# An attention stage with its score products on 64 rows, its query unstacked and its values between zeros

## The chip, the cores and the metric

The kernel runs on one core of a Trainium2 chip. Its time is that of one launch on the device, in microseconds (us); the time shown is the median of several runs. A profile is one execution that the hardware profiler took. It names the engines PE (TensorE; PEld is its weight loads), DVE (VectorE), ACT (ScalarE), POOL (GpSimd) and SP (SyncE, which here only starts transfers).

## What is computed

An encoder trunk of two layers on 256 tokens of width 1024: each layer is a SwiGLU, a mixer, and a SwiGLU again, each followed by a layer norm. The mixer of the first layer is an mLSTM, that of the second is attention in a window, and only the attention is changed here. It has 16 query heads of size 64 and 4 key heads; four query heads share a key head. Each query sees keys up to 128 tokens away, with a penalty that grows with the distance, and each head has a sink in the denominator. Cut to that:

```python
D_MODEL, SEQ, HEAD_DIM, N_Q_HEADS, N_KV_HEADS, WINDOW = 1024, 256, 64, 16, 4, 128

def window_attention(x, w_in, sink, w_out):
    p = x @ w_in                                   # q, k, v
    ...
    s = jnp.einsum('bnqkgd,bnskd->bnkgqs', q, kw).astype(jnp.float32) * (HEAD_DIM ** -0.5)
    ...
    s = s - slopes[:, :, None, None] * dist
    s = jnp.where(valid[None, :, None, None], s, MASK_VALUE)
    m = jnp.maximum(jnp.max(s, axis=-1, keepdims=True), sink_l)
    pe = jnp.exp(s - m)
    attn = pe / (jnp.sum(pe, axis=-1, keepdims=True) + jnp.exp(sink_l - m))
    o = jnp.einsum('bnkgqs,bnskd->bnqkgd', attn, vw.astype(jnp.float32)).reshape(B, S, nq)
    return o.astype(x.dtype) @ w_out
```

## The kernel before

Six stages follow one another (FFN, mLSTM, FFN, FFN, attention, FFN), and the whole of it is issued from lists. The functions of the stages do not issue instructions, they record them: `Program` collects every operation, and `Program.issue` gives them out in the order of the list `ORDER` (steps between indices of the recorded operations), the same order for all engines. Which buffer of a rotating group an operation uses is written out as well, in `SLOTS`, one digit per use. Both lists were made ahead for the whole kernel. So the order of the program text sets what depends on what, and the lists set how the work of neighbouring steps is interleaved.

All matrix products work on numbers split in two: a value x is kept as hi (x rounded to fp32r) and lo (the rest, x - hi, also fp32r). A product is three matmuls, hi*hi, hi*lo and lo*hi (`mm3`). A split out of a PSUM bank (`split_evac`) is a cast on ScalarE for hi and a subtraction on VectorE for lo. Weights come in as words of 128 x 1024 by the SP queue, wait in rooms for raw weights, and are split by ScalarE and VectorE into a ring of ten (`w_hi`, `w_lo`).

The attention stage (`attn`) works with heads in pairs: pair j holds heads 2j and 2j+1 (called a = 0 and 1), and pairs 2g and 2g+1 share key head g. t counts the two blocks of 128 queries, sb the two blocks of 128 keys.

- `proj`, `k_turn`, `q_turn` and `q_rest` project keys, values and the query, and turn keys and query so that the head's 64 dimensions lie on the partitions. Of a pair's query, head a = 0 then lies on partitions 0 to 63 and head a = 1 on 64 to 127. The keys are put on both halves of the partitions, twice the same.
- `stacked` puts the query of one head into `q2` with hi on partitions 0 to 63 and lo on 64 to 127. One matmul on 128 rows with the doubled keys hi thus gives (hi + lo) * hi; a second one with the keys lo gives the rest. For each head that is one cast on ScalarE and one subtraction on VectorE, each on 64 partitions.
- `scores(j)` takes two PSUM banks, one per query block t, each with both heads side by side. A matmul with the distances (512 columns) opens each bank, four score matmuls of 256 columns follow, and one `reduce_max` on VectorE reads the bank. Small operations make the bias, then four exponentials on ScalarE read the banks.
- `scale(j)` divides by the sum on GpSimd; `turn(j, sb)` transposes on TensorE and splits the result into `pr` (cast now, subtraction with the next `flush`).
- `values(j)` multiplies: the weights are the 128 columns [values hi | values lo] of key head g (tile `va`, `v0` and `v1` in the trace), the moving operand is `pr` hi or lo of both heads, 512 columns, for both key blocks: four matmuls into one bank of 128 x (2, 256). In it, head a = 0 has its hi part on partitions 0 to 63 and its lo part on 64 to 127 of columns 0 to 255, head a = 1 likewise in the other columns. Two copies on ScalarE and two additions on VectorE bring them together in the tile `o`, which is then split into `q2` in the place of the pair's query.
- `out_proj` multiplies that with the output weights, into four PSUM banks that stay taken until the end of the stage. `q_rest` in the first steps and `out_proj` in the later ones are put between as filling.

The loop over `st` runs eleven steps; step st works on the scores of pair st, the scaling of pair st-1, the turning of pair st-2 and the values of pair st-3. PSUM has eight banks in one group (`p`). The stage has six rooms for raw weights, the four common ones and two of its own (`s_raw`).

Of the kernel before, what the change touches and what calls it, by code (L numbers as in the profile page):

```python
# [259 lines left out]
        "792047126847"),  # L260
    "t.0": ("20315553143105122040201230230"),
    "stats": ("110100101010"),
    "mv": ("010011111111"),
    "rs": ("101101010000"),
    "raw.1": ("31030310310213023021012301201320"),
    "wt.1": ("1023"),
# [167 lines left out]
def trunk_kernel(ctx: ExitStack, tc: tile.TileContext, x, ffn_w_in, ffn_w_out, ln_g, ln_b, ml_w_in, ml_gate_b,  # L434
# [207 lines left out]
    def tok(t):  # L642
        return slice(t * 128, (t + 1) * 128)
# [849 lines left out]
```

## Time and profile before

| what | value |
|---|---|
| median of 3 runs | 922.61 us (922.59 to 923.38) |
| the profiled execution | 922.74 us, span of its instructions 921.0 us |
| granted TensorE clock, mean | 0.998 |
| instructions | 12305 |
| VectorE, ScalarE, GpSimd busy | 89%, 63%, 15% of the span |
| read from HBM, written | 206.65 MB, 1.05 MB |
| attention stage | its projections and its last output products lie at about 640 and 738 us |

How to read it: TensorE's instructions overlap one another, so a matmul's own duration is longer than the time from its start to the next one's, and the busy share says little about how densely they follow. A row of the timeline gives start, duration, engine, line, operation, out<-in, the used part of the array, the moving operand's shape and the count; in square brackets stands the idle time in front and what ended it. A row of the groups gives the same kind of names, the count, the busy time with the mean in ns, and the idle time in front. All rows name line 314, the one at which `issue` gives out every operation; so they are told apart by the names of their tiles: out<-in, moving operand first, weights last. `sc` are the exponentials, `pr_hir` and `pr_lor` the turned ones, `q2r` the query and, later, the result, `kk` the keys, `distr` the distances, `p` a PSUM bank.

### The profile page before, as it was taken

What the parts mean: (1) busy time and instruction counts of PE and PEld (TensorE: products, weight loads), DVE (VectorE), ACT (ScalarE), POOL (GpSimd) and SP (SyncE); (2) the same over time, 40 slices, a digit from 0 to 9 for tenths busy, and PEclk for the clock granted to TensorE, in tenths of its full rate; (3) what the DMA queues carried; (4) which work ended last, traced back from release to release, by engine and by line L of the source; (5) the groups of instructions that cost most, each with busy time, mean ns of one, the idle gap of its engine ahead of it and who ended that gap; (6) DMA issues with size and microseconds to landing.
All of it is one profiled execution on the core that took longest, in us unless ns stands there. A gap on an engine that the chain in (4) does not pass through costs nothing.

```text
span 921.0 us, 12305 instructions
## 1 busy us (share of the span) xinstructions
PE 907.0 (98%) x4381; PEld 753.3 (82%) x4381; DVE 818.0 (89%) x964; ACT 580.7 (63%) x818; POOL 142.5 (15%) x198
## 2 busy tenths in 40 slices
PE   8999999999999999999999999999999999999996
PEld 6888888889988888888888888888887788888885
DVE  6999899887789999889999989898899799988986
ACT  6767577445754667566637675675589567666660
POOL 0111121210111112111011112010335311202110
PEclk9999999999999999999999999999999999999999
DMA  9998999567344888899968898976751278998951
GB/s 333 299 242 268 274 283 242 186 203 230 141 168 167 282 249 187 287 262 249 323 224 203 237 289 243 288 184 203 235 202 67 93 228 235 260 305 199 310 131 46
DMA packets 100654, 208.51 MB, mean 226 GB/s; under 512 B 6864, under 2 KB 21216, under 8 KB 100592
## 3 DMA queue, kind: packets, MB, share of 16 engines
q1 hardware_dynamic: 82816, 173.82, 53.7%
q0 software_dynamic: 17632, 33.64, 22.0%
q8 instruction: 34, 0.56, 0.2%
q10 hardware_dynamic: 144, 0.26, 0.1%
q14 instruction: 28, 0.23, 0.1%
HBM read 206.65 MB, written 1.05 MB: 226 GB/s over the span
## 4 chain that ended last, share of the span: by engine, by line
PE 95%; DVE 2%; ACT 1%; DMA 1%; issue 0%; POOL 0%; DVEq 0%; ACTq 0%; SPq 0%; POOLq 0%
PE p L314 95%; DMA w_raw<-in_at_w_out_dram 1%; ACT sc L314 1%; DVE rm L314 1%; DMA x<-in_x_dram 0%; DVE pr_lor L314 0%; DVE x L314 0%; ACT xT_hi L314 0%; ACT pr_hir L314 0%; DVE q2r L314 0%; POOL sc L314 0%; ACT q2r L314 0%; POOL sm L314 0%; DVE nm L314 0%; DVE o L314 0%
## 5 line engine op out<-in xcount | busy, mean ns | idle before, releaser
L314 ACT CAST w_hi<-s_raw 128x1024 fp32r<-128x1024 f32 x243 | 249.6, 1052 | 96.7 <-PE p L314 60.5
L314 DVE TENSOR_TENSOR w_lo<-s_raw,w_hi 128x1024 fp32r<-128x1024 f32 x243 | 289.5, 1219 | 17.3 <-ACT w_hi L314 15.7
L314 ACT CAST w_hi<-w_raw 128x1024 fp32r<-128x1024 f32 (+1 forms) x163 | 168.1, 1042 | 82.2 <-PE p L314 41.4
L314 DVE TENSOR_TENSOR w_lo<-w_raw,w_hi 128x1024 fp32r<-128x1024 f32 (+1 forms) x163 | 194.9, 1210 | 22.1 <-ACT w_hi L314 15.7
L314 PE MATMUL p<-w_hi,xT_hi 128*128 128x512 f32 x512 | 197.8, 396 | 1.3 <-ACT xT_hi L314 0.9
L314 PE MATMUL p<-w_lo,xT_hi 128*128 128x512 f32 x512 | 196.3, 393 | 0.5 <-DVE w_lo L314 0.5
L314 PE MATMUL p<-w_hi,xT_lo 128*128 128x512 f32 x512 | 195.8, 392 | 0.0
L314 PE MATMUL p<-w_hi,h_hir 128*128 128x512 f32 (+1 forms) x323 | 119.6, 392 | 0.0
L314 PE MATMUL p<-w_hi,h_lor 128*128 128x512 f32 (+1 forms) x323 | 118.0, 389 | 0.0
L314 PE MATMUL p<-w_lo,h_hir 128*128 128x512 f32 (+1 forms) x323 | 117.8, 389 | 0.0
L314 PEld LDWEIGHTS p<-w_hi,xT_hi 128*128 128x128 f32 x512 | 96.1, 188 | 21.3 <-ACT xT_hi L314 1.6
L314 PEld LDWEIGHTS p<-w_lo,xT_hi 128*128 128x128 f32 x512 | 96.2, 188 | 19.7 <-DVE w_lo L314 0.9
L314 PEld LDWEIGHTS p<-w_hi,xT_lo 128*128 128x128 f32 x512 | 96.0, 188 | 19.8 <-DVE xT_lo L314 0.9
L314 PE MATMUL p<-w_lo,S_hir 128*128 128x512 f32 x256 | 97.3, 389 | 0.0
L314 PE MATMUL p<-w_hi,S_hir 128*128 128x512 f32 x256 | 96.5, 390 | 0.0
L314 POOL DMA_DIRECT2D s_raw<-in_ffn_w_in_dram x41 | 50.5, 1274 | 291.4 <-DVE w_lo L314 135.2
L314 PE MATMUL p<-w_hi,S_lor 128*128 128x512 f32 x256 | 95.5, 389 | 0.0
L314 PEld LDWEIGHTS p<-w_lo,h_hir 128*128 128x128 f32 x323 | 60.7, 188 | 12.2
L314 PEld LDWEIGHTS p<-w_hi,h_lor 128*128 128x128 f32 x323 | 60.7, 188 | 12.1
L314 PEld LDWEIGHTS p<-w_hi,h_hir 128*128 128x128 f32 x323 | 60.6, 188 | 12.0 <-issue 0.2
L314 POOL DMA_DIRECT2D w_raw<-in_ffn_w_in_dram x23 | 28.9, 1274 | 196.2 <-DVE s_raw L314 74.5
L314 PEld LDWEIGHTS p<-w_hi,S_hir 128*128 128x128 f32 x256 | 48.1, 188 | 10.5 <-ACT t L314 0.6
(195 smaller groups left out, 1220.7 us busy)
## 6 DMA issues: line engine op xcount, KB each, us to landing
s_raw<-in_ffn_w_in_dram SPq DMA_DIRECT2D x103, 512.0 KB, 6.5
s_raw<-in_ffn_w_out_dram SPq DMA_DIRECT2D x57, 512.0 KB, 6.3
w_raw<-in_ffn_w_in_dram SPq DMA_DIRECT2D x56, 512.0 KB, 5.3
s_raw<-in_ffn_w_in_dram POOLq DMA_DIRECT2D x41, 512.0 KB, 7.4
w_raw<-in_ffn_w_out_dram SPq DMA_DIRECT2D x31, 512.0 KB, 6.1
w_raw<-in_ml_w_in_dram SPq DMA_DIRECT2D x24, 512.0 KB, 4.1
w_raw<-in_ffn_w_in_dram POOLq DMA_DIRECT2D x23, 512.0 KB, 7.4
s_raw<-in_ffn_w_in_dram SPq DMA_DIRECT2D x18, 256.0 KB, 5.9
```

The costliest lines, as they stand in the source:

```text
L314: f(*args, **kw)
```

## The change

The query is no longer stacked: `stacked` goes, and one cast and one subtraction on 128 partitions put both heads of a pair into `q2`, hi and lo as two slices. A score product of a head is then three matmuls on 64 rows (hi*hi, hi*lo, lo*hi; the product lo*lo, which the stacking brought along, is not computed any more), on partitions 0 to 63 for a = 0 and on 64 to 127 for a = 1. The two heads are issued in turn. The two banks are now one per head, with both query blocks in it; both are opened by their distances first, and the two `reduce_max` follow when all twelve matmuls are done.

The tile of the values is [hi or lo][576 columns]: nine strips of 64, the values of the four key heads in strips 1, 3, 5 and 7, zeros in the others, filled once by GpSimd. Two neighbouring strips are the weights, [values | zeros] for a = 0 and [zeros | values] for a = 1, so that the two heads come out on partitions 0 to 63 and 64 to 127 of the same 256 columns. Twelve matmuls of 256 columns (three products, two key blocks, two heads) add up in one bank. The copies, the additions and the tile `o` go; the split reads the bank. Since the values take more room, the stage has one raw room of its own instead of two.

`ORDER` (6641 operations before, 6697 after) and all of `SLOTS` are made anew, for the whole kernel.

```diff
@@ the lists
-    "0 10 -9 10 -9 11 -10 11 -5 6 1 -12 13 1 -13 14 1 -14 15 1 -15 16 1 1 1 -18 21 1 -3 92 -88 1 3 102 -109 5 1 "
...
-    "raw.4": ("05121212150432104215"),
+    "raw.4": ("02124141341203402134"),
...
-    "o.4": ("01001001"),
@@ attn
-            va = [tile_([128, 4, 2, 64], FR, f"v{t}") for t in range(2)]
+            va = [tile_([128, 2, 576], FR, f"v{t}") for t in range(2)]
+            for v in va:
+                for e in range(2):
+                    nc.gpsimd.memset(v[:, e].bitcast(F32).rearrange("p (g d) -> p g d", d=64)[:, 0::2], 0.0)
             q2 = tile_([128, 8, 2, S], FR, "q2")
-            rooms.kind(f"raw.{keys[bound[0]]}", raws + pool.new("s_raw", D, 2, F32))
+            rooms.kind(f"raw.{keys[bound[0]]}", raws + pool.new("s_raw", D, 1, F32))
@@ proj
-                    split_evac((va[t][:, :, 0], va[t][:, :, 1]), kv[:, 1])
+                    split_evac(tuple(va[t][:, e].rearrange("p (g d) -> p g d", d=64)[:, 1::2] for e in range(2)), kv[:, 1])
@@ the query
-            def stacked(j, a, m, src, scale=None):
-
-                r = slice(64 * a, 64 * a + 64)
-                split_evac((q2[0:64, j, a, m], q2[64:128, j, a, m]), src[r], scale[r] if scale is not None else None)
-
             def q_turn(t):
                 p = ybank((128, 4, 128))
                 for j in range(4):
                     nc.tensor.transpose(p[:, j], qd[t][:, j], ident)
-                for a in range(2):
-                    stacked(slice(0, 4), a, tok(t), p)
+                split_evac((q2[:, 0:4, 0, tok(t)], q2[:, 0:4, 1, tok(t)]), p)
@@ q_rest
-                        for a in range(2):
-                            stacked(4 + 2 * g + f, a, A, p, qs_col[:, 2 * g + f:2 * g + f + 1])
+                        j = 4 + 2 * g + f
+                        split_evac((q2[:, j, 0], q2[:, j, 1]), p, qs_col[:, j - 4:j - 3])
@@ scores
+                for a in range(2):
+                    nc.tensor.matmul(ps[a], neg_id, dist, start=True, stop=False)
                 for t in range(2):
-                    p = ps[t]
-                    nc.tensor.matmul(p, neg_id, dist[:, t, None, :].to_broadcast([128, 2, S]), start=True, stop=False)
-                    for a in range(2):
-                        for e in range(2):
-                            nc.tensor.matmul(p[:, a], q2[:, j, a, tok(t)], kk[e][:, g], start=False, stop=a == e == 1)
-                    nc.vector.reduce_max(rm[:, t], p, axis=AX.X)
+                    for n_, (qe, ke) in enumerate(((0, 0), (0, 1), (1, 0))):
+                        for a in range(2):
+                            r = slice(64 * a, 64 * a + 64)
+                            nc.tensor.matmul(ps[a][:, t], q2[r, j, qe, tok(t)], kk[ke][r, g], start=False,
+                                             stop=t == 1 and n_ == 2)
+                for a in range(2):
+                    nc.vector.reduce_max(rm[:, :, a], ps[a], axis=AX.X)
...
-                        nc.scalar.activation(s_[:, a], ps[t][:, a], AF.Exp, bias=nm[:, t, a:a + 1],
+                        nc.scalar.activation(s_[:, a], ps[a][:, t], AF.Exp, bias=nm[:, t, a:a + 1],
@@ values
-                p = wbank((128, 2, S))
-                for e in range(2):
-                    for sb in range(2):
-                        v = va[sb][:, j // 2].rearrange("p a d -> p (a d)")
-                        nc.tensor.matmul(p, v, pr[j, sb][e], start=e == sb == 0, stop=e == sb == 1)
-                o = tile_([128, S], F32, "o", bufs=2)
-                top, low = slice(0, 64), slice(64, 128)
-                nc.scalar.copy(o[top], p[top, 0])
-                nc.scalar.copy(o[low], p[low, 1])
-                nc.vector.tensor_add(o[top], p[low, 0], o[top])
-                nc.vector.tensor_add(o[low], p[top, 1], o[low])
-                sums[j] = o
+                p, g = wbank((128, S)), j // 2
+                for n_, (ve, pe, sb) in enumerate((ve, pe, sb) for ve, pe in ((0, 0), (1, 0), (0, 1)) for sb in range(2)):
+                    for a in range(2):
+                        v = va[sb][:, ve, 64 * (2 * g + 1 - a):64 * (2 * g + 3 - a)]
+                        nc.tensor.matmul(p, v, pr[j, sb][pe][:, a], start=n_ == a == 0, stop=n_ == 5 and a == 1)
+                sums[j] = p
```

More of the change, by code (lines that the diff above doesn't have):

```diff
@@ L40 @@
     "0 10 -9 10 -9 11 -10 11 -5 6 1 -12 13 1 -13 14 1 -14 15 1 -15 16 1 1 1 -18 21 1 -3 92 -88 1 3 102 -109 5 1 "
[202 rows of a table removed]
[207 rows of a table added]
 )
 SLOTS = {
-    "raw.0": ("310284657392ab105846a2b0183547691837250843691a72b5639a1057b22a480152"),
-    "p": ("2361465267076413642572050257052727205203204216104257346125643410720315412735704762031032627145603150"
-        "4264317175057055107050171142061751740651736662040264420066204241201267251243267315610234607154062714"
-        "0525265663256632563236371250342507143621515077051105707150177"),
@@ L249 @@
-    "h_hir.0": ("10101"),
-    "h_lor.0": ("10010"),
-    "w_hi": ("3759063987516238248506728136740289256013953748250349107285436910723548619024578361259047836125904837"
-        "6129503874612950387614295081734659280716534298017653297690134826075183694207518369420751836940721398"
-        "5642187039564218709365421876903452183765932186304675934218095763421809573642581907632489750613872495"
-        "0163782410956378241059637824015963782041695378426907184685947218936074821569730481625973840162793615"
-        "243261708934"),
@@ L256 @@
-    "w_lo": ("0694569384254036594617051398472830452143692780153976214085373649015823091657382041593678402159368047"
-        "1250897416235089743201569473812065942017236049357412461829305749482153409267918342560714908653170864"
-        "3257834906123578496102537894712753041894293674914765430854193265754819360528479316204591067439201856"
-        "3479201345968701345296780145639287416357920741563425890274910876832910287614592015736402197862340518"
-        "792047126847"),
-    "t.0": ("20315553143105122040201230230"),
@@ L262 @@
[L262 to L266, printed above, removed]
-    "a_hir.1": ("1010"),
-    "a_lor.1": ("1010"),
-    "den.1": ("1101"),
-    "hst.1": ("1011"),
-    "hmv.1": ("0010"),
-    "hrs.1": ("0001"),
-    "h_hir.2": ("0100110101"),
-    "h_lor.2": ("1000101001"),
-    "raw.2": ("95684731250476983a1b6a48795312b07952a08619b3457ba039284b676598104ba5761304b1a0536924b1786094213b578a"
-        "21370b46518a23970b81a3276904305b2764"),
@@ L277 @@
-    "t.2": ("1204305412031340301344210350441201354210311452005242345344"),
-    "sc.4": ("1024351350425012354035"),
-    "raw.4": ("05121212150432104215"),
-    "rm.4": ("10211212"),
-    "nm.4": ("00012112"),
-    "sm.4": ("12001202"),
-    "es.4": ("20122102"),
-    "pr0_hir.4": ("10100110"),
-    "pr0_lor.4": ("11010101"),
-    "pr1_hir.4": ("11100011"),
-    "pr1_lor.4": ("00000000"),
-    "o.4": ("01001001"),
-    "h_hir.5": ("01110"),
-    "h_lor.5": ("01101"),
-    "raw.5": ("32b0350217495a86230ba7598361042b8364a08b1327596704a32b5906874b094571"),
@@ L292 @@
-    "t.5": ("00430521330431420453415033415"),
+    "raw.0": ("123057846291ba305784a3b0271645981725360742891a53b6829b1354a03b763150"),
+    "p": ("4132063675273606435512752752172575271710516750235027645201235360417356041703162574604757302453173457"
+        "0410362762525622765767255747620613046052067313747431714343741712757034301520567014625370236145320615"
+        "3477204772047720407274001275465702317564234204024320440243341"),
+    "h_hir.0": ("01001"),
+    "h_lor.0": ("01010"),
+    "w_hi": ("4065397312604987253617829036527483416709517832519046738251460793825046153924089617403528961407352689"
+        "1407386592417038652491703861524970386519847025139684720831649578120965374820619534782061953748206315"
+        "9748150263978415029763841507962834179056283456792810346572936581497023658149706235849106578124095368"
+        "7421095376482109536748210953468721095684712396805479168543760298675183026475918307642591830746250853"
+        "401752968074"),
@@ new lines @@
+    "w_lo": ("7391405042319405351946372089640578315862787481329754052983654190236957498314827059152368170945628317"
+        "9405236178945023671589402369871502349765408267391547231906825340186198213704695837025491368904516850"
+        "4921546703985421679308541265348219654031784320390618217453201397417682564087951236845907968071238594"
+        "1276038954126079358412607953248167593804359680241304862361945079284627015972568407512839045172634075"
+        "920859307462"),
+    "t.0": ("10314023012314231354153010143"),
@@ new lines @@
+    "stats": ("100011010001"),
+    "mv": ("010100100011"),
+    "rs": ("111101101100"),
+    "raw.1": ("31020211202310110320312031031203"),
+    "wt.1": ("1203"),
+    "a_hir.1": ("0101"),
+    "a_lor.1": ("1101"),
+    "den.1": ("1010"),
+    "hst.1": ("0111"),
+    "hmv.1": ("1001"),
+    "hrs.1": ("1110"),
+    "h_hir.2": ("0101001010"),
+    "h_lor.2": ("1010110110"),
+    "raw.2": ("4856790315284679063ba849765130b27650819a36b2754081b60472985ab431729a8532653280a6971432b596741032a85b"
+        "0138a05641b92378a0b19238675a3040386a"),
@@ new lines @@
+    "t.2": ("2412205344014523451220325513525014203154051244542013021503"),
+    "sc.4": ("3404251345305410452310"),
+    "raw.4": ("02124141341203402134"),
+    "rm.4": ("21121210"),
+    "nm.4": ("21002201"),
+    "sm.4": ("20112121"),
+    "es.4": ("10112111"),
+    "pr0_hir.4": ("00100111"),
+    "pr0_lor.4": ("00100111"),
+    "pr1_hir.4": ("10010000"),
+    "pr1_lor.4": ("00000110"),
+    "h_hir.5": ("01001"),
+    "h_lor.5": ("10101"),
+    "raw.5": ("0123105328407639ab5170623ba594813ba425078a496231b51a97438b6228534b05"),
@@ L293 @@
+    "t.5": ("00410540050423423531151202045"),
 }
```

409 rows, old and new, of the table ORDER are left out of this document.

## The prediction

> **What bounds the kernel now.** I read the page first, then the busy time by stretches of 10 us around the attention stage, then TensorE's instructions in order of time there, and last what TensorE waited for.
>
> ```profile
> span 921.0 us, 12305 instructions
> ...
> PE 907.0 (98%) x4381; PEld 753.3 (82%) x4381; DVE 818.0 (89%) x964; ACT 580.7 (63%) x818; POOL 142.5 (15%) x198
> ```
>
> TensorE is busy for 98% of the span, so over the whole kernel any work that is added to it is paid for. The attention stage lies at about 640 to 738 us, and in its middle the picture is another one:
>
> ```profile
> core 0: us, PE busy (x) PEld busy (x) DVE busy (x) ACT busy (x) POOL busy (x), PEclk, DMA share, GB/s
> 640.00:650.00 10.00, 10.00 (x49) 8.35 (x49) 8.98 (x14) 4.24 (x5) 1.47 (x1) 1.00 0.34 99
> ...
> 660.00:670.00 10.00, 10.00 (x50) 8.30 (x49) 9.50 (x10) 7.86 (x11) 0.00 (x0) 1.00 0.58 184
> ...
> 690.00:700.00 10.00, 9.34 (x59) 7.35 (x57) 9.64 (x20) 9.89 (x31) 6.16 (x13) 1.00 0.20 71
> ...
> 710.00:720.00 10.00, 9.12 (x52) 6.85 (x50) 7.26 (x17) 8.33 (x30) 4.73 (x10) 1.00 0.00 1
> ```
>
> At 690 to 700 us ScalarE is busy for 9.89 and VectorE for 9.64 of 10 us, while TensorE has gaps. So in the eight steps of the heads' loop three engines are nearly full at once, and it is TensorE that waits a little for the other two. The granted clock is 1.00 throughout, so it plays no part.
>
> ```profile
> PE p L314 <- DVE pr_lor L314: 1.1, 3, 0.7
> PE p L314 <- ACT pr_hir L314: 0.7, 1, 0.7
> PE p L314 <- POOL sc L314: 0.6, 1, 0.6
> PE p L314 <- ACT q2r L314: 0.3, 1, 0.3
> PE p L314 <- ACT sc L314: 0.2, 1, 0.2
> ```
>
> These are all waits of TensorE between 670 and 730 us (total, times, longest): 2.9 us in 7 waits, of which 2.3 us end with ScalarE or VectorE. The true loss is somewhat larger, because the modelled end of a matmul covers the start of the gap:
>
> ```profile
> 709.72 0.60 PE L314 MATMUL p<-ident,sc 128*128 128x128 f32 x4
> 710.08 0.48 PE L314 MATMUL p<-w_lo,q2r 128*128 128x512 f32 x1
> 710.39 0.39 PE L314 MATMUL p<-pr_hir,v0r 128*128 128x512 f32 x1
> ...
> 711.34 0.40 PE L314 MATMUL p<-pr_lor,v0r 128*128 128x512 f32 x1
> ...
> 711.95 0.63 PE L314 MATMUL p<-ident,sc 128*128 128x128 f32 x4 [0.22 <-DVE pr_lor L314]
> ```
>
> Here 0.61 us lie between two starts where 0.23 is usual (next fence): 0.38 lost, and 0.22 shown as idle, 0.16 more per wait. With 7 waits the loss is 2.9 + 7 x 0.16 = 4.0 us. That is the most that lighter ScalarE and VectorE work can give back on this engine.
>
> **The change part by part.** What a matmul costs is read from start to start, not from its own duration:
>
> ```profile
> 701.14 0.39 PE L314 MATMUL p<-w_hi,q2r 128*128 128x512 f32 x1
> 701.37 0.40 PE L314 MATMUL p<-distr,neg_id 128*128 128x512 f32 x1
> ...
> 701.83 0.28 PE L314 MATMUL p<-kk_hir,q2r 128*128 128x256 f32 x1
> 701.95 0.28 PE L314 MATMUL p<-kk_lor,q2r 128*128 128x256 f32 x1
> 702.06 0.28 PE L314 MATMUL p<-kk_hir,q2r 128*128 128x256 f32 x1
> 702.18 0.28 PE L314 MATMUL p<-kk_lor,q2r 128*128 128x256 f32 x1
> ```
>
> A matmul of 512 columns takes 0.23 us, one of 256 takes (702.18 - 701.83) / 3 = 0.117, with its weights loaded behind the one before.
>
> *Values.* Per pair of heads four matmuls of 512 columns become twelve of 256 on the full array (three products, two key blocks, two heads). 12 x 0.117 - 4 x 0.23 = 0.48 us; eight pairs: **+3.9 us** of TensorE. This term has its rows and hardly a bound to either side.
>
> *Scores.* Per pair eight matmuls of 256 columns on 128 rows become twelve of 256 columns on 64 rows, the two heads on the two halves of the array in turn; the two matmuls with the distances stay at 512 columns each. No matmul in the trace runs beside another on the other half of the rows, so the price has to be bounded. Lower bound: two halves go side by side, six times 0.117 = 0.70 against 8 x 0.117 = 0.94, that is -0.24 a pair, -1.9 us in all. Upper bound: one after the other, 12 x 0.117 = 1.40, +0.46 a pair, +3.7 us. The nearest rows are the transposes in the fence above: four of them take 0.36 us up to the next matmul, and that next one 0.31 instead of 0.23. A transpose streams 128 columns, a quarter of 512, yet costs 0.09 to 0.11; so what sets it is not its columns but, as I read it, the load of its 128 columns of weights, and a load that isn't hidden shows as the 0.08 behind the group. A score matmul of 64 rows still loads 128 columns. If loads follow each other at 0.11, twelve take 1.31: +0.37 a pair, **+3.0 us**. I take this value.
>
> *Entering and leaving the half array.* The trace has two short groups with 64 rows, the transposes of the gates in the mLSTM stage:
>
> ```profile
> 212.60 0.28 PE L314 MATMUL p<-xT_hi,w_hi 128*128 128x256 f32 x1
> 212.72 0.28 PE L314 MATMUL p<-xT_lo,w_hi 128*128 128x256 f32 x1
> 212.93 0.33 PE L314 MATMUL p<-ident,fe 64*128 64x64 f32 x2
> 213.19 0.38 PE L314 MATMUL p<-xT_hi,w_lo 128*128 128x256 f32 x1
> 213.41 0.28 PE L314 MATMUL p<-xT_hi,w_hi 128*128 128x256 f32 x1
> ```
>
> The step into the group is 0.21 instead of 0.12, the step after it 0.22 instead of 0.12: 0.19 us per group. It is a bound from above, since they are transposes too; the bound from below is nothing. The program writes a pair's twelve score matmuls as one group, so eight groups: **+1.5 us**.
>
> The Trainium skill bears this row out in TensorEngine Tiling (Array Packing), Key Properties: changing the tiling mode, not merely the tile, drains TensorE. The rule speaks against the change; without it the sum would be 1.5 us less. The same section says that different tiles may load weights and multiply in parallel, which would give the lower bound of the scores; no run so far shows it.
>
> *ScalarE and VectorE.* These instructions go or are halved:
>
> ```profile
> L314 POOL TENSOR_SCALAR sc<-sc,sm 128x256 f32<-128x256 f32 x32 | 15.0, 487 | 0.9
> ...
> L314 DVE TENSOR_REDUCE rm<-p 128x2 f32<-128x512 f32 x16 | 10.6, 687 | 0.6 <-PE p L314 0.4
> ...
> L314 DVE TENSOR_TENSOR o<-p,o 64x256 f32<-64x256 f32 x16 | 6.8, 422 | 0.7 <-ACT o L314 0.3
> ...
> L314 ACT COPY o<-p 64x256 f32<-64x256 f32 x16 | 5.9, 370 | 1.6 <-PE p L314 1.4
> ...
> L314 DVE SCALAR_TENSOR_TENSOR q2r<-p,qs_col,q2r 64x256 fp32r<-64x256 f32 x8 | 3.9, 484 | 0.7 <-ACT q2r L314 0.5
> L314 ACT ACTIVATE q2r<-p,qs_col 64x256 fp32r<-64x256 f32 x8 | 3.8, 472 | 0.1
> ...
> L314 DVE TENSOR_TENSOR q2r<-p,q2r 64x512 fp32r<-64x512 f32 x4 | 2.7, 690 | 0.1
> ...
> L314 ACT CAST q2r<-p 64x512 fp32r<-64x512 f32 x4 | 2.3, 580 | 1.2 <-DVE q2r L314 0.8 <-PE p L314 0.4
> ```
>
> All 16 copies and 16 additions of the sum fall away, and half of the query's evacuations, because one instruction on 128 rows replaces two on 64. ScalarE: 16 x 0.370 + 4 x 0.472 + 2 x 0.580 = 9.0 us less. VectorE: 16 x 0.422 + 4 x 0.484 + 2 x 0.690 = 10.1 us less. Both were nearly full at 690 to 700 us, so the waits of TensorE that end with them should shrink, also the wait for the split output (q2r) behind the sum. I give back their share of the loss, 4.0 x 2.3 / 2.9 = **-3.2 us** (bounds: nothing, and the whole 4.0). What is late next is the step on GpSimd that scales the exponentials (0.6 us of the waits), and TensorE itself.
>
> *The row maximum.* The 16 reductions stay at 0.687. Before, the first of a pair could start when half of the matmuls were done; now both banks close only at the end of the group, so the chain from scores to exponentials gets up to 0.69 us longer per pair. Behind the maximum stand VectorE's next splits and behind those the exponentials on ScalarE. I take nothing: the steps are staggered by one pair of heads, and TensorE has transposes, values and projection of other pairs to go on with. With that cover gone it costs 8 x 0.69 = 5.5 us.
>
> *Zeros, rooms, bank.* Four fills of 320 columns are new on GpSimd, about 0.6 each by the 0.487 for 256 columns (an estimate): 2.4 us, with GpSimd idle from 660 to 670 us: nothing. One of six rooms for raw weights goes; transfers take only 0.20 and 0.00 of the engines' time at 690 to 700 and 710 to 720 us, so I take nothing, and if a load does come late it is one landing:
>
> ```profile
> w_raw<-in_at_w_out_dram SPq DMA_DIRECT2D x6, 512.0 KB, 5.3
> ```
>
> at most 5.3 us once. The values' bank is now read by the split directly instead of by copies and additions: it is free no later than before. The new lists move instructions in all stages, but outside attention TensorE already shows 10.00 of 10 us (640 to 650), so nothing is to be gained there, and I put nothing on it.
>
> **Sum.** 3.9 + 3.0 + 1.5 - 3.2 = +5.2 us. The profiled execution took 922.74 us, its span of 921.0 and 1.74 around it, 0.13 above the median of 922.61. So 922.61 + 5.2 = **927.8 us**.
>
> **The rivals.** *The two halves run side by side* (the other side: not slower). Place: the score groups; price: 0.117 for two matmuls in place of 0.22, so the scores give -1.9 instead of +3.0: 3.9 - 1.9 + 1.5 - 3.2 = +0.3, 922.9 us. If the entering then costs nothing as well and the whole 4.0 is given back: 3.9 - 1.9 - 4.0 = -2.0, 920.6. It decides as soon as a pair of score matmuls starts within about 0.15 us. For it: the two heads write to different banks and use different rows. Against it: the spacing of the transposes. The Trainium skill, TensorE: Matmul & The Clock Gate, Part 3, reports such packing with starts about 4 ns apart; by that rule this rival would be the forecast, and the trace so far neither shows nor excludes it.
>
> *The score groups are cut up.* In the order before, the score matmuls alternate with matmuls of the projections, and the new list may do so too. With four groups a pair instead of one there are 32 entries and exits at 0.19, 6.1 us instead of 1.5: 932.4 us. For it: nearly nothing else can fill the waits. Against it: the 0.19 belongs to transposes.
>
> *A new wait instead of the old ones.* Later maxima, both score banks held longer while four of eight banks belong to the output projection: nothing is given back and about 2 us (some of the 5.5) come on top, 927.8 + 3.2 + 2 = 933 us. Against it: ScalarE and VectorE, which stand behind, have 9 to 10 us less to do.
>
> **How the numbers follow.** Forecast 0.44, halves side by side 0.36, groups cut up 0.13, new wait 0.07. A change of 0.2%, 1.85 us, is about what can be told here. The rival with the halves side by side spreads from 919 to 925: faster 0.20, same 0.10, slower 0.06. The forecast's own range is 924 to 931, with tails: faster 0.04, same 0.05, slower 0.35. The other two are slower, 0.20. Together faster 0.24, same 0.15, slower 0.61. The range from 919.8 to 932.8 leaves out a little of the fastest and of the slowest cases.
>
> **What would show it.** Score matmuls of 64 rows 0.11 to 0.12 apart, and 0.2 where a group begins or ends, speak for the forecast; pairs within some hundredths for the first rival. Value matmuls should stand 0.117 apart, twelve a pair. The waits of TensorE for pr_hir, pr_lor and q2r should fall well below 2.3 us, ScalarE and VectorE show some 9 and 10 us less between 660 and 740 us, and TensorE no gaps in the middle. The prediction is wrong if the waits stay, or if the time moves in another stage.

## The result, and the profile after

The changed kernel takes 930.21 us (median of 4 runs, 929.83 to 930.51) against 922.9 us (922.59 to 923.38): a ratio of 1.0079, 95% interval 1.0061 to 1.0096, 7.3 us slower. The profiled execution took 929.83 us with a span of 928.1. From the page of after:

```profile
span 928.1 us, 12464 instructions
...
PE 917.4 (99%) x4477; PEld 762.8 (82%) x4477; DVE 807.8 (87%) x942; ACT 570.3 (61%) x796; POOL 143.2 (15%) x202
```

Against the same row of before, VectorE has 10.2 us less (818.0 to 807.8) and ScalarE 10.4 us less (580.7 to 570.3), while TensorE is busy for 10.4 us more. The change lies where it was expected: from the first matmul with the distances to the last output product before takes 65.8 us (672.31 to 738.12) and after 72.1 us (672.51 to 744.60), so 6.3 of the 7.1 us between the two spans arise there. Two of the stretches of 10 us of after:

```profile
690.00:700.00 10.00, 10.00 (x80) 8.97 (x79) 8.21 (x16) 8.02 (x22) 5.18 (x11) 1.00 0.01 2
...
710.00:720.00 10.00, 10.00 (x66) 8.15 (x65) 7.08 (x14) 6.32 (x20) 6.11 (x12) 1.00 0.31 104
```

TensorE has no gap left in the middle of the stage, and the view of its waits between 670 and 736 us, which had five rows before, has none. The relief did arrive, and the waits are gone, whether by the relief or because TensorE has more to do; the experiments tell these apart. And yet the kernel is slower, so TensorE must be doing more, or slower, work. Its order of time in after shows which:

```profile
700.26 0.28 PE L318 MATMUL p<-pr_lor,v0r 128*128 128x256 f32 x1
700.47 0.39 PE L318 MATMUL p<-kk_lor,q2r 64*128 64x256 f32 x1
700.47 0.50 PE L318 MATMUL p<-kk_hir,q2r 64*128 64x256 f32 x2
700.69 0.28 PE L318 MATMUL p<-kk_lor,q2r 64*128 64x256 f32 x1
700.81 0.39 PE L318 MATMUL p<-kk_hir,q2r 64*128 64x256 f32 x3
700.93 0.28 PE L318 MATMUL p<-kk_lor,q2r 64*128 64x256 f32 x1
701.14 0.39 PE L318 MATMUL p<-pr_lor,v1r 128*128 128x256 f32 x1
701.36 0.38 PE L318 MATMUL p<-ident,sc 128*128 128x128 f32 x2
701.67 0.38 PE L318 MATMUL p<-kk_hir,q2r 64*128 64x256 f32 x1
701.68 0.39 PE L318 MATMUL p<-kk_lor,q2r 64*128 64x256 f32 x1
701.90 0.28 PE L318 MATMUL p<-kk_hir,q2r 64*128 64x256 f32 x1
...
705.91 0.40 PE L318 MATMUL p<-distr,neg_id 128*128 128x512 f32 x1
706.24 0.38 PE L318 MATMUL p<-kk_hir,q2r 64*128 64x256 f32 x1
706.55 0.51 PE L318 MATMUL p<-pr_hir,v0r 128*128 128x256 f32 x2
706.89 0.40 PE L318 MATMUL p<-pr_hir,v1r 128*128 128x256 f32 x2
```

Two things are to be read here. First, the score matmuls of the two heads start together (two at 700.47): the halves of the array do run side by side, and after the first pair a pair takes about 0.12 us (700.69, 700.81, 700.93). In the trace, partners start at most 9 ns apart, mostly 3 or 4. Second, the new list cuts the pairs of heads into pieces. A group of eight begins at 700.47 and ends before 701.14; its steps are 0.21 into it (0.12 usual), 0.22 for its first pair, 0.21 out of it. At 706.24 a single score matmul stands alone: 0.33 us since the distances' matmul (0.23 usual), 0.31 to the next one, and 0.34 for the two after that (0.24 usual). It costs 0.10 + 0.31 + 0.10 = 0.51 us of TensorE, where a matmul of 256 columns on 128 rows cost 0.12. All 96 score matmuls stand in 27 such groups. Added up over them: 3.5 us lost in front, 4.6 between the first and the last start of a group, 7.0 from a group's last start to the next matmul, 1.6 lost behind, together 16.8 us before rounding; the 64 score matmuls of before took 64 x 0.119 = 7.6 us.

The values are as expected: twelve of 256 columns a pair, 0.12 apart. The rows of their groups by form, between 640 and 760 us of after:

```profile
L318 PE MATMUL p<-pr_hir,v0r 128*128 128x256 f32 x32 | 7.9, 294 | 0.0
L318 PE MATMUL p<-pr_hir,v1r 128*128 128x256 f32 x32 | 7.3, 290 | 0.0
...
L318 PE MATMUL p<-pr_lor,v1r 128*128 128x256 f32 x16 | 4.7, 311 | 0.0
...
L318 DVE TENSOR_REDUCE rm<-p 128x2 f32<-128x512 f32 x16 | 10.4, 688 | 9.2 <-PE p L318 9.0
...
L318 POOL MEMSET v0r<- 128x320 f32 x2 | 0.7, 362 | 0.0
L318 POOL MEMSET v1r<- 128x320 f32 x2 | 0.7, 356 | 0.0
```

VectorE now sits idle for 9.0 us ahead of the row maxima, until TensorE has closed the banks (0.4 of it before). As no wait of TensorE shows behind it, no cost of it can be seen here. The new fills take 1.4 us of GpSimd.

### The profile page after: what moved, and what is told of

Read it like the earlier page. It is cut to its first block, busy times and chain, and to the rows that moved or that the text cites. A ratio compares the mean times of both kernels' runs of the same rounds, so it can differ in the third digit from the quotient of the medians.

```text
span 928.1 us, 12464 instructions
## 1 busy us (share of the span) xinstructions
PE 917.4 (99%) x4477; PEld 762.8 (82%) x4477; DVE 807.8 (87%) x942; ACT 570.3 (61%) x796; POOL 143.2 (15%) x202
## 4 chain that ended last, share of the span: by engine, by line
PE 98%; DVE 0%; DMA 0%; ACT 0%; issue 0%; DVEq 0%
PE p L318 98%; DMA x<-in_x_dram 0%; DVE x L318 0%; ACT xT_hi L318 0%; DVEq L1487 0%; DVE w_lo L318 0%; DVE stats L318 0%; DVE mv L318 0%; DVE neg_id L318 0%; DVE rs L318 0%; DVE xT_lo L318 0%; DVEq L318 0%
## 5 line engine op out<-in xcount | busy, mean ns | idle before, releaser
L318 PE MATMUL p<-w_hi,xT_hi 128*128 128x512 f32 x512 | 195.0, 395 | 0.9 <-ACT xT_hi L318 0.9
L318 PE MATMUL p<-w_hi,h_lor 128*128 128x512 f32 (+1 forms) x323 | 120.1, 390 | 0.0
L318 POOL DMA_DIRECT2D s_raw<-in_ffn_w_in_dram x43 | 53.0, 1275 | 308.4 <-DVE w_lo L318 90.1
L318 PEld LDWEIGHTS p<-w_hi,S_hir 128*128 128x128 f32 x256 | 48.1, 188 | 10.1 <-ACT t L318 0.2
L318 PEld LDWEIGHTS p<-w_hi,S_lor 128*128 128x128 f32 x256 | 48.1, 188 | 10.0
```

What stands on the lines that cost most here:

```text
L318: f(*args, **kw)
```

## The experiments

Theory A: the halves run side by side, and what makes the kernel slower is that each group of 64 rows pays for entering and leaving, 27 times. Theory B: cutting costs little, and the values' additional columns are the price. Each experiment has the kernel before timed beside it; its median lay at 922.7 to 923.0 us.

To move instructions, the issuing loop of these kernels can hold a run of operations together, at the place of the last of them; operations that are left out keep an empty place, so that the rest of the list stays as it is (the lists have 6678 operations in before and 6734 in after, not the 6641 and 6697 given with the change; the difference is 56 either way):

```diff
+        for run, then in self.runs:
+            at = max(order.index(i) for i in run)
+            early = [i for i in order[:at] if i in then]
+            rest = [i for i in order[:at] if i not in run and i not in then]
+            order = rest + list(run) + early + order[at + 1:]
```

**The score matmuls of a pair together** (from after):

```diff
+                n0 = len(nc.ops)
                 for t in range(2):
                     for n_, (qe, ke) in enumerate(((0, 0), (0, 1), (1, 0))):
...
+                nc.runs.append((range(n0, n0 + 12), (n0 + 12, n0 + 13)))
```

> The kernel after, with the twelve score matmuls of a pair of heads issued one behind the other, at the place of the last of them; nothing else is changed. Theory A (the two halves of the rows run side by side, and each group pays for entering and leaving): in the trace of after the 96 score matmuls stand in 27 groups, and with what they delay in front and behind they take 16.8 us of TensorE; the one whole group there takes 0.71 inside, 0.21 to the next start and about 0.1 in front and behind, 1.12 us. Eight such groups take 9.0, so 7.8 us less: 922.4 us, and 924 if TensorE then waits a little for the later data. Theory B (cutting costs little, the values alone make the kernel slower): 930 us, no change.

Measured: 924.74 us (11 runs), ratio to before 1.0016 [1.0007, 1.0024]; 5.5 us less than after, by nothing but the places of the score matmuls (and of one row maximum that stood between them). TensorE in order of time:

```profile
701.59 0.28 PE L323 MATMUL p<-pr_lor,v1r 128*128 128x256 f32 x1
701.81 0.39 PE L323 MATMUL p<-kk_hir,q2r 64*128 64x256 f32 x2
702.03 0.28 PE L323 MATMUL p<-kk_lor,q2r 64*128 64x256 f32 x2
702.15 0.40 PE L323 MATMUL p<-kk_hir,q2r 64*128 64x256 f32 x4
702.39 0.28 PE L323 MATMUL p<-kk_lor,q2r 64*128 64x256 f32 x2
702.50 0.28 PE L323 MATMUL p<-kk_hir,q2r 64*128 64x256 f32 x2
702.72 0.73 PE L323 MATMUL p<-w_hi,q2r 128*128 128x512 f32 x2
703.29 0.60 PE L323 MATMUL p<-ident,sc 128*128 128x128 f32 x4
```

Twelve score matmuls run in 702.72 - 701.81 = 0.91 us, of which the first pair takes 0.22, the next four about 0.12 each, and from the start of the last pair to the next full matmul it is 0.21; about 0.10 in front and 0.10 behind come on top. The eight groups take 8.8 us instead of 16.8. Of these 8.0 us 5.5 reach the time. TensorE's waits over the whole span show new ones at two places:

```profile
PE p L323 <- DVE h_lor L323: 0.7, 1, 0.7
PE p L323 <- DVE pr_lor L323: 0.7, 2, 0.5
...
PE p L323 <- ACT h_hir L323: 0.4, 1, 0.4
```

The wait for `pr_lor` lies in the attention stage, which is still 6.7 us shorter than in after (65.4 us from the first distances to the last output product) and even 0.4 us shorter than in before. The two waits for `h` lie at 874 to 878 us, in the last FFN: ScalarE's cast of h stands there behind the casts of two weight words, the first of which landed 11.2 us after its issue (8.6 us for the same word in after). Behind the attention stage this execution takes 185.1 us, that of after 183.5. Why the word came late, and whether it does in every run, isn't known; the fastest of the 11 runs took 923.62 us.

So theory A holds, and B falls. The number I had given for no waits (922.4) was too low; the 924 that allowed for them was near, though part of the waits lie in another stage than was meant.

**One head, then the other** (from the grouped kernel; the loop over a is moved outside):

```diff
-                for t in range(2):
-                    for n_, (qe, ke) in enumerate(((0, 0), (0, 1), (1, 0))):
-                        for a in range(2):
-                            r = slice(64 * a, 64 * a + 64)
+                for a in range(2):
+                    r = slice(64 * a, 64 * a + 64)
+                    for t in range(2):
+                        for n_, (qe, ke) in enumerate(((0, 0), (0, 1), (1, 0))):
```

> As the grouped kernel, but within the group first the six score matmuls of one head, then the six of the other, so that neighbours use the same half of the rows. Theory A: neighbours on the same half follow one another at 0.119, as single ones do in the trace of after (starts 0.118 and 0.120 apart at the end of the group of ten), so twelve take 1.43 instead of 0.71, 8 x 0.71 = 5.7 us more than the grouped kernel: 928 us. If the order of the heads doesn't matter, because the hardware holds both halves anyway: as the grouped kernel.

Measured: 927.15 us (5 runs), 1.0049 [1.0035, 1.0063], 2.4 us above the grouped kernel where I had expected 5.7.

```profile
703.44 0.38 PE L323 MATMUL p<-kk_hir,q2r 64*128 64x256 f32 x1
703.67 0.28 PE L323 MATMUL p<-kk_lor,q2r 64*128 64x256 f32 x1
703.78 0.39 PE L323 MATMUL p<-kk_hir,q2r 64*128 64x256 f32 x3
704.01 0.28 PE L323 MATMUL p<-kk_lor,q2r 64*128 64x256 f32 x2
704.13 0.40 PE L323 MATMUL p<-kk_hir,q2r 64*128 64x256 f32 x3
704.37 0.28 PE L323 MATMUL p<-kk_lor,q2r 64*128 64x256 f32 x1
704.49 0.28 PE L323 MATMUL p<-kk_hir,q2r 64*128 64x256 f32 x1
704.69 0.73 PE L323 MATMUL p<-w_hi,q2r 128*128 128x512 f32 x2
```

The group takes 704.69 - 703.44 = 1.25 us instead of 0.91: "in turn" is worth 0.34 us a pair of heads. It isn't the full doubling, because the second head's matmuls begin before the first head's are through. In the trace the six of the first head start from 703.44 to 704.14 and the six of the second from 703.79 to 704.49, each at 0.22 for the first step and 0.12 from then on; three times in the middle two start within 5 to 7 ns of each other.

**The values as before** (from after; four matmuls together at the place of the last of the twelve, and the copies and additions ahead of the cast, on ScalarE and VectorE):

```diff
-                for n_, (ve, pe, sb) in enumerate((ve, pe, sb) for ve, pe in ((0, 0), (1, 0), (0, 1)) for sb in range(2)):
-                    for a in range(2):
-                        v = va[sb][:, ve, 64 * (2 * g + 1 - a):64 * (2 * g + 3 - a)]
-                        nc.tensor.matmul(p, v, pr[j, sb][pe][:, a], start=n_ == a == 0, stop=n_ == 5 and a == 1)
+                for e in range(2):
+                    for sb in range(2):
+                        v = va[sb][:, j // 2].rearrange("p a d -> p (a d)")
+                        nc.tensor.matmul(p, v, pr[j, sb][e], start=e == sb == 0, stop=e == sb == 1)
...
+                    nc.scalar.copy(o[top], p[top, 0])
+                    nc.scalar.copy(o[low], p[low, 1])
+                    nc.vector.tensor_add(o[top], p[low, 0], o[top])
+                    nc.vector.tensor_add(o[low], p[top, 1], o[low])
...
                     nc.scalar.copy(d[0], o)
```

> The kernel after with the values as before: four matmuls of 512 columns per pair, issued together at the place of the last of the twelve, then two copies on ScalarE and two additions on VectorE ahead of the cast; scores and query stay as after. Theory A: TensorE has 12 x 0.119 - 4 x 0.233 = 0.50 us less per pair, 3.9 us in all, and is the only bound: 926.2 us. Rival (the relief of ScalarE and VectorE is what matters): 5.9 and 6.8 us come back on them, the waits of TensorE come back with up to 4 us, and the time stays at 930.

Measured: 947.0 us (4 runs), 1.0256 [1.0239, 1.0273]. The same with the scores grouped:

> Grouped scores and the values as before, both edits at once; what stays of the change is the query that isn't stacked and the three products on 64 rows. Theory A: 930.2 - 7.8 - 3.9 = 918.5 us if no waits come back, 922 if they come back in full (4 us, as in the kernel before); either way not slower than before. Theory B: 926 us, as with the values alone.

Measured: 939.61 us (4 runs), 1.0173 [1.0157, 1.019]. Both miss every expectation, and neither tells what the values cost. TensorE's waits in the first of the two between 670 and 740 us (up to 760 us those for `q2r` add up to 5.0):

```profile
PE p L323 <- DVE pr_lor L323: 4.3, 4, 1.8
PE p L323 <- POOL sc L323: 3.6, 3, 2.2
PE p L323 <- ACT q2r L323: 1.5, 1, 1.5
```

The list of after leaves only 3 to 18 places between the last value matmul of a pair and the cast. Into that I put copies and additions that wait for one another across two engines, so, as I read the waits, the queues stood still behind them, the later heads' turned exponentials included; no run separates this. That a list made for one program is unfit for another is all that follows. The grouping is again worth some 7 us between the two (947.0 to 939.6). I went over to the order of before and took single parts of the change into it.

**The relief alone** (from before; no sum, and the split reads the bank at the places of the copies and additions):

```diff
-                nc.scalar.copy(o[top], p[top, 0])
-                nc.scalar.copy(o[low], p[low, 1])
-                nc.vector.tensor_add(o[top], p[low, 0], o[top])
-                nc.vector.tensor_add(o[low], p[top, 1], o[low])
+                nc.scalar.copy(q2[:, j, 0], p[:, 0])
+                nc.blank(1)
+                nc.vector.tensor_sub(q2[:, j, 1], p[:, 0], q2[:, j, 0].bitcast(F32))
+                nc.blank(1)
```

> The kernel before without the sum of the values' parts: the two copies on ScalarE and the two additions on VectorE per pair are left out, and the cast and the subtraction read the bank's first 256 columns directly, at the places of the copies and additions (so the output lacks parts of each head). The relief alone: 5.9 us less on ScalarE, 6.8 on VectorE, nothing added. By the step of the prediction, waits of TensorE of 4.0 us of which a share of 2.3/2.9 ends with these engines: up to 3.2 us less, 919.7 us; with two thirds of the relief, 2.1 us less, 920.9. Rival (TensorE's own work and the order set the time): 923.0 us, no change.

Measured: 922.2 us (11 runs), 0.9996 [0.9987, 1.0005]: no gain that can be told. TensorE's waits between 670 and 740 us:

```profile
PE p L319 <- POOL sc L319: 0.6, 1, 0.6
PE p L319 <- POOL neg_slope L319: 0.6, 1, 0.6
PE p L319 <- DVE pr_lor L319: 0.6, 2, 0.4
PE p L319 <- ACT sc L319: 0.2, 1, 0.2
```

The waits for the split results shrink (2.3 us end with ScalarE or VectorE in before, 0.8 here), but others remain or come in, 2.0 us in all against 2.9.

**The values' part alone** (from before; zeros, twelve matmuls at the places of the four, split as above):

```diff
...
+                for pe in range(2):
+                    for sb in range(2):
+                        for ve in range(2 - pe):
+                            for a in range(2):
+                                v = va[sb][:, ve, 64 * (2 * g + 1 - a):64 * (2 * g + 3 - a)]
+                                nc.tensor.matmul(p, v, pr[j, sb][pe][:, a], start=pe == sb == ve == a == 0, stop=pe == sb == a == 1)
+                        nc.merge(4 - 2 * pe)
```

> The values' part of the change alone, in the kernel before with its order: zeros beside the values, twelve matmuls of 256 columns at the places of the four, cast and subtraction read the bank at the places of the copies and additions; scores and query as before. Values cost 8 x (12 x 0.119 - 4 x 0.233) = 4.0 us more on TensorE, and the relief of the kernel without the sum comes off: 923.0 + 4.0 - 2.1 to 3.2 = 923.8 to 924.9 us. If waits hide the added matmuls: 921 to 922. If the relief is worth nothing: 927.

Measured: 922.62 us (11 runs), 0.9997 [0.9988, 1.0006]. By their number and spacing the matmuls are 4.0 us more of TensorE, and the time stays. TensorE's waits between 670 and 740 us are 1.3 us, against 2.9 in before:

```profile
PE p L319 <- POOL sc L319: 0.6, 1, 0.6
PE p L319 <- DVE pr_lor L319: 0.5, 1, 0.5
PE p L319 <- ACT sc L319: 0.2, 1, 0.2
```

That leaves two readings: the matmuls fill gaps that are there anyway, or the relief pays for them. To tell them apart,

**the values' part without its relief**: the copies and additions stay at their places and write a tile that nobody reads.

```diff
+                nc.scalar.copy(o[top], p[top])
+                nc.scalar.copy(o[low], p[low])
                 nc.scalar.copy(q2[:, j, 0], p)
...
+                nc.vector.tensor_add(o[top], p[top], o[top])
+                nc.vector.tensor_add(o[low], p[low], o[low])
                 nc.vector.tensor_sub(q2[:, j, 1], p, q2[:, j, 0].bitcast(F32))
```

> The values' part alone, as in the kernel with the zeros alone, but with the two copies and two additions per pair kept at their places (they read the bank and write a tile that nobody uses), so that ScalarE and VectorE are as full as before: 4.0 us of TensorE more and no relief. Theory C (the added matmuls fill gaps of TensorE that are there anyway, and the relief is worth about nothing, as in the kernel without the sum): 922.5 to 923.5 us. Theory D (the relief paid for the matmuls): 925 to 927 us.

Measured: 926.58 us (5 runs), 1.0043 [1.003, 1.0057]. Without the relief the twelve matmuls cost 926.58 - 922.65 = 3.9 us, with it 4.0 less (926.58 - 922.62). That is theory D. TensorE's waits here, the first row a new one, 2.8 us in all:

```profile
PE p L319 <- DVE nm L319: 1.2, 1, 1.2
PE p L319 <- DVE pr_lor L319: 0.8, 2, 0.5
PE p L319 <- POOL sc L319: 0.6, 1, 0.6
PE p L319 <- ACT sc L319: 0.2, 1, 0.2
```

The size is less sure than the medians make it. In the kept execution 2.5 of its 3.9 us more than before lie between the first distances and the last output product (68.3 us; 65.7 with the relief); 0.4 lie ahead of them, and 0.9 behind the last matmul, where the last write of the output landed 7.5 us after it instead of 6.5. Whether the other runs have that too isn't known. So the relief is worth 2.7 to 4.0 us where TensorE has as much more to do, which still is theory D, and by itself 0.5 us, which isn't clear of noise. My reading is that what it frees can be used only if TensorE has work for it. The rows name the waits; which of them turned the one into the other was not taken apart further. The relief is also more than busy time: with the copies and additions in place, the cast and the subtraction stand behind them.

**Grouping without the 64 rows** (from before; the eight score matmuls of a pair together, as a control):

```diff
+                nc.runs.append(([n0 + i for i in (1, 2, 3, 4, 7, 8, 9, 10)], (n0 + 5, n0 + 11)))
```

> Control for the grouping: the kernel before with the eight score matmuls of a pair issued together at the place of the last. On 128 rows a group has nothing to enter or leave: theory A expects no change from this on TensorE, 923 us, and some waits more, since the first reduction can't start early any more (up to 0.7 us a pair, if nothing covers it: 928). If grouping itself is what made the grouped kernel faster, 5 us less here too: 918.

Measured: 924.58 us (8 runs), 1.0022 [1.0012, 1.0032]. Grouping by itself makes the kernel slower by 1.9 us, and TensorE's waits between 670 and 740 us grow from 2.9 to 4.2; so the 5.5 us of the first experiment are not a virtue of grouping but of the entries and exits that it spares.

**Scores and query alone** (from before, in groups; values as before):

```diff
...
+                nc.tensor.matmul(ps[0], neg_id, dist, start=True, stop=False)
+                nc.blank(5)
+                nc.tensor.matmul(ps[1], neg_id, dist, start=True, stop=False)
+                for t in range(2):
+                    for n_, (qe, ke) in enumerate(((0, 0), (0, 1), (1, 0))):
+                        for a in range(2):
+                            r = slice(64 * a, 64 * a + 64)
+                            nc.tensor.matmul(ps[a][:, t], q2[r, j, qe, tok(t)], kk[ke][r, g], start=False,
+                                             stop=t == 1 and n_ == 2)
+                nc.merge(12)
...
```

> The scores' and the query's part of the change alone, in the kernel before with its order, as groups: query unstacked, one bank per head, twelve matmuls on 64 rows in turn at the place of the last of the eight; values as before. Groups of 64 rows took 8.8 us of TensorE in the grouped kernel, the eight matmuls on 128 rows take 8 x 8 x 0.119 = 7.6: 1.2 us more; 3.1 us less on ScalarE and 3.3 on VectorE, worth about 1 us: 923.2 us. If the later row maximum is a new wait, it shows here: up to 5.5 us more, 928.5.

Measured: 924.52 us (11 runs), 1.002 [1.0011, 1.0028], 1.8 us slower, as much as the control. TensorE's waits are 4.1 us here, nearly those of the control. I read it so that the 1.1 us more of TensorE and the lighter ScalarE and VectorE about cancel and what is left is the closed group with what it delays, as in the control; this fits the numbers, but the parts were not run one by one.

**The same lesson on the transposes.** The step behind a group of transposes costs 0.08 more too, and the 64 of the turns stand in 33 groups in before. In the kernel with the zeros alone, and in the kernel before, the four transposes of a turn were held together:

```diff
+                nc.runs.append((range(n0, n0 + 4), ()))
```

> The kernel with the zeros alone, and the four transposes of each turn issued together at the place of the last: 33 groups of transposes become 16 at most, and the step behind a group costs 0.08 to 0.09 more: up to 17 x 0.085 = 1.4 us less, 921.2 us; since TensorE has few waits left there, a good part of it should show. If the later transposes are waited for: 923 or more. This would be the version that beats both kernels.

> The same grouping of the transposes in the kernel before, without anything of the change: up to 1.4 us less if TensorE's own time counts there, 921.5 us; 922.7 to 924 if the waits that remain take it up, as they did with the relief alone.

Measured: 923.42 us (11 runs), 1.0008 [0.9999, 1.0017], and 923.18 us (11 runs), 1.0008 [0.9999, 1.0017]. Neither gains anything. What the fewer groups would spare is at most 1.4 us by the prediction's rows. The waits of TensorE for the exponentials (ACT `sc`) grow from 0.2 us to 1.2 in the first and 1.4 in the second, which fits that issuing the early transposes later takes the gain back. No whole kernel here beats the one before. Both parts of the change together in the order of before were not run, so what the new order does by itself stays open.

## Why the prediction was right, and where it was not

The time lay 2.4 us above the forecast (927.8 to 930.21), within its range, and its direction and size were right. Its steps were not all right. The sum held because two errors in the scores went opposite ways: as TensorE's time the scores were forecast at 3.0 + 1.5 = 4.5 us more and took 16.8 - 7.6 = 9.2, and more was given back than the 3.2 us put against it. That the time still came out within the range is in good part luck.

*Values, +3.9:* right. Twelve a pair stand 0.119 apart, and 3.9 us were measured with ScalarE and VectorE as full as before, of which the kept execution shows 2.5 in the attention stage.

*Relief, -3.2:* right in size where it counts, 4.0 us measured together with the values' matmuls (2.7 in the attention stage). Wrong as a term by itself: alone it brings 0.5 us, not clear of noise. The prediction took waits that end with an engine for waits that vanish with that engine's load; in these runs they gave way to other waits unless TensorE had other work. The loads fell much as worked out (VectorE 10.1 forecast and 10.2 measured over the span, ScalarE 9.0 and 10.4).

*Scores, +3.0:* this step failed. I put the price at 0.11 a matmul from the spacing of the transposes, reading that as the load of the weights, one after another. On 64 rows the matmuls of two halves start mostly 3 or 4 ns apart and the next pair 0.12 later: a whole group takes 0.70 from its first to its last start, where 1.31 was forecast for the twelve. Inside a group the rival "side by side" is what happens; the transposes' spacing says nothing about two halves. The Trainium skill reports such packed matmuls starting about 4 ns apart (TensorE: Matmul & The Clock Gate, Part 3), and the trace agrees.

*Entering and leaving, +1.5:* the second step that failed, in number more than in price. Eight groups were assumed because the program text writes them so; the list makes 27 of them. A group costs about 0.10 in front, 0.10 more for its first pair, 0.1 more on the way out (0.2 where the whole group is one pair or a single, which then has no first step to pay) and 0.1 behind, so 0.4 rather than 0.19. The Trainium skill's rule that a change of the tiling mode drains TensorE (TensorEngine Tiling (Array Packing), Key Properties) agrees in kind; the page gives no price, and these rows do. I had written down both facts as rivals that exclude each other, "side by side" and "cut up", with 0.36 and 0.13. They are true together, and the price of the second is far above the gain of the first.

*Row maximum, 0:* in after it costs nothing that can be seen, though VectorE waits 9.0 us for the closed banks. In the order of before, as in the control with grouping, a closed group with what it delays costs 1.9 us.

*Zeros, rooms, bank, 0:* right as far as the parts go: the zeros with their matmuls and the relief sum up to nothing, and TensorE shows no wait for a weight in the attention stage of after. The single raw room itself was not tried; whether it has a part in the late weight word of the grouped kernel stays open.

*The sum, put together from the runs:* values +3.9, relief -4.0, scores and query in whole groups +1.8, cutting +5.5 (930.2 - 924.7): +7.2, against 7.3 measured. That it fits so well is in part chance. The first three come from the order of before, where TensorE waits, and the last from the order of after, where it doesn't, and the traces (one execution each) lay the time elsewhere:

| kernel | median, us | first distances to last output product, us |
|---|---|---|
| before | 922.7 | 65.8 |
| values' part alone | 922.6 | 65.7 |
| values' part without its relief | 926.6 | 68.3 |
| scores and query alone, in groups | 924.5 | 67.7 |
| after, score matmuls grouped | 924.7 | 65.4 |
| after | 930.2 | 72.1 |

The grouped kernel's 1.7 us above before are therefore not the 1.8 of the scores and the query: in its attention stage it takes no more time than before, and most of what it loses it loses behind it. What holds by the stage too is the price of cutting, 6.7 us there. One thing is left open: TensorE's rows give 4.0 us more for the values and 9.2 for the scores, less the 4.0 of the waits 9.2 in all, and the stage grew by 6.3. That the transposes stand in 26 groups instead of 33 is a part of the difference; the rest was not taken apart.

## What to carry to other kernels

If matmuls on half the rows are used to run two at a time, issue them as one closed run and alternate the halves: cut into 27 groups, 96 of them took 16.8 us, in 8 groups 8.8. A list or a planner that interleaves them freely must know the 0.4 us of a group. And a lighter helper engine was worth something here only together with more work for the bound engine; price the two together, not one by one.

## What the runs showed of the hardware that was not expected

The two halves of the array work off their matmuls as two streams: even when six of one half are followed by six of the other, the second half's first starts 0.35 us after the first half's first, ahead of three matmuls that come earlier in the program, and twelve take 1.25 us up to the next full matmul instead of 0.91 in turn. And a lone matmul of 64 rows between matmuls of 128 rows, with what it delays, costs 0.51 us, four times a matmul of 256 columns on the full array.
